# A planned two-layer RWKV-7/RetNet trunk: due-time schedules, ordered loads, and an inverse that reads its blocks from a padded copy in DRAM

## The chip, the cores and the metric

The kernel runs on one core of one Trainium2 chip. The metric is device time in microseconds (us), the median of several executions. Five engines matter: PE (TensorE, the matrix multiplier), DVE (VectorE), ACT (ScalarE), POOL (GpSimd) and SP (SyncE), which here only issues DMAs. Each engine works through its own instructions strictly in order; an instruction that waits holds up all that stand behind it on its engine, and a DMA that waits on SP holds up all later DMAs of SP.

## The reference

The input x is 256 tokens of 1024 features. Two layers each do

```
x += 1/2 swiglu(rms_norm(x))            # "f1"
h  = rms_norm(x);  proj = h @ w_in      # "mix": 1792 columns for RWKV, 1536 for RetNet
x += [rwkv7(proj_a) | retnet(proj_b)] @ w_out
x += 1/2 swiglu(rms_norm(x))            # "f2"
```

and a last rms_norm follows. swiglu is silu(h @ w_gate) * (h @ w_up) @ w_down with 2816 inner features. RWKV-7 has 8 heads of 64 and a state that each token updates: S <- S*diag(w) + (S a) b^T + v k^T, y = S r. The kernel does it in chunks of 64 tokens, and for each chunk and head it needs the inverse of a 64 x 64 unit triangular matrix. RetNet has 4 heads, with decay masks inside a chunk and between chunks.

## The kernel before

The 256 tokens are two tiles of 128, t0 and t1. Each runs as a stream of steps, and both share every weight: a weight half (128 x 1024 fp32, 512 KB) is loaded by SP into one of three raw buffers, ACT writes its rounded copy `hi`, DVE writes the remainder `lo`, and PE makes three products for each block (hi*hi, hi*lo, lo*hi). There are 332 halves: 66 for each f1, 34 for each mix (26 for the seven input projections, 8 for the output projection) and 66 for each f2. 22 places for hi and lo hold eleven halves at once.

In the mix the projections are m (decay, loras), k, r, q, e, g and v, in that order of loading; then come, for each tile: `R` (RetNet core), `J` (merge), `a` and `b` (the two chunks), `c` (closing norm) and the output projections `W` (RetNet half) and `w` (RWKV half). After r, `rwkv_receptance` forms the triangular matrices `el` (2 chunks x 4 head pairs, 128 partitions x 64 columns each) and calls `inverse`, which inverts their sixteen-wide diagonal blocks: the 64 blocks go through DRAM (`d1`) so that each comes to lie on one partition (`mx`), DVE doubles the inverted width from 2 to 4, 8 and 16, and the result goes back through DRAM (`d2`) into `xc`, which lies in the tile named misc. `merge` (J) joins the blocks to full inverses in four PE steps (`pre`), with ACT and DVE between them. Chunk steps a and b (`ch`) follow one another through the state `sv`; t1's follow t0's.

Nothing in this order is written by hand. The program is recorded as nodes, a planner (`Plan`) prices every node, computes each node's longest way to the end (`tails`), and simulates a list schedule with the priorities way + guide * position, for each of seven guides; the priorities with the earliest simulated end give the order in which every engine's instructions are emitted. A node that is recorded with `in_turn()` keeps its place among all nodes so marked; the weight loads are marked, the loads of x and of the constants are not.

Names in the rows: `base` holds x, constants, small vectors and the raw weight buffers; `wide` the hi and lo places; `parts` the normalized, transposed x; `gu` a bank for gate/up, projections and output projections; `acc` the banks of the down projection; `rh`, `rl` and `mh`, `ml` the inputs of W and w. Nearly all instructions carry the line of one helper, so the tiles tell them apart.

Of the kernel before, what the change touches and what calls it, by code (L numbers as in the profile page):

```python
# [21 lines left out]
P = 128  # L22
# [19 lines left out]
NPAIR = 4  # L42
# [108 lines left out]
class Op:  # L151
    __slots__ = ("eng", "call", "args", "kw", "outs", "ins", "cost", "late", "node", "at", "n", "form")


class Node:


    def __init__(self, eng):
        self.eng, self.ops, self.preds, self.succs = eng, [], {}, []
        self.touched = []  # L160
        self.dur = 0.0
        self.form = None


# [14 lines left out]
class Plan:  # L179
# [34 lines left out]
    def in_turn(self):  # L214

        n = self.nodes[-1]
        if self.turn is not None:
            n.preds.setdefault(self.turn, TURN)
        self.turn = n

    def record(self, eng, call, args, kw):
# [61 lines left out]
    def price(self, op):  # L283
# [36 lines left out]
        elif eng == "vector":  # L320
            if call == "tensor_tensor_scan":
                op.cost = 1224.0
            elif call in ("tensor_scalar", "tensor_copy", "memset") and not psum:
                op.cost = 150 + 0.52 * n
            elif call == "tensor_reduce":
                op.cost = 151 + 1.04 * int(np.prod(op.args[1].shape[1:]))
            elif len(out.shape) > 3 and out.shape[0] == 64:
                op.cost = 150 + 1.77 * n
            else:
                op.cost = 151 + 1.04 * n + (63 if col else 0)  # L330
        else:
            op.cost = 600.0 if call == "memset" else 450 + 190.0 * n
        op.cost += 20
# [14 lines left out]

    def tails(self, arcs):

        order = sorted(self.nodes, key=lambda n: (n.start, n.i)) if arcs else self.nodes
        tail = [0.0] * len(self.nodes)
        for n in reversed(order):
            best = n.dur
            for s, lag in n.succs:
                v = (60 if lag is TURN else lag) + tail[s.i]
                if v > best:
                    best = v
            for s, lag in (arcs.get(n.i, ()) if arcs else ()):
                v = (60 if lag is TURN else lag) + tail[s.i]  # L360
                if v > best:
                    best = v
            tail[n.i] = best
        return tail

    def simulate(self, prio):

        import heapq
        nodes = self.nodes
# [3 lines left out]
        state = {0: (128, 128), 2: "s"}  # L373
        lastnode = [None] * 5
        arcs = {}
        waiting = [[] for _ in range(5)]
        ready = [[] for _ in range(5)]
        places = {k: [(0.0, i, None) for i in range(n)] for k, (n, _) in PLACES.items()}
        left = {}
# [14 lines left out]
        while done < total:  # L394
# [6 lines left out]
            while pending and pending[0][0] <= t:  # L401
                ft, _, b, n = heapq.heappop(pending)
                places[b.space].append((ft, b.place, n))
            for e in range(5):
# [28 lines left out]
                for b in new:  # L433
                    pool = places[b.space]
                    j = min(range(len(pool)), key=lambda k: pool[k][0])
                    ft, b.place, prev = pool.pop(j)
                    if prev is not None:
                        arcs.setdefault(prev.i, []).append((n, max(1.0, ft - prev.start)))
                    low[b.space] = min(low.get(b.space, 99), len(pool))
# [11 lines left out]
                dur = n.dur + extra  # L451
                if lastnode[e] is not None:
                    arcs.setdefault(lastnode[e].i, []).append((n, t - lastnode[e].start if False else lastnode[e].real))
                lastnode[e] = n
                n.real = dur
# [25 lines left out]
                for b in n.touched:  # L481
                    b.last = max(b.last, fin + 60)
                    left[b.i] -= 1
                    if not left[b.i]:
                        heapq.heappush(pending, (b.last, b.i, b, n))
                        heapq.heappush(events, b.last)
        return end, arcs

    def schedule(self):

        self.prepare()
        way, n = self.tails(None), len(self.nodes)
        best = None
        for guide in GUIDES:
            prio = [w + guide * (n - i) * 1e5 / n for i, w in enumerate(way)]
            try:
                end, _ = self.simulate(prio)
            except Stuck:
                continue
            if best is None or end < best[0]:  # L500
                best = (end, prio)
            if VERBOSE:
                print(guide, end, self.low)
        self.end, _ = self.simulate(best[1])

# [38 lines left out]
class Trunk:  # L544
# [145 lines left out]
    def ffn(self, t, col, base, pause=()):  # L690
# [14 lines left out]
        for b in range(NB):  # L705
# [183 lines left out]
    def rwkv_receptance(self, t, ps):  # L889
# [12 lines left out]
        misc = A.get([P, 512], "misc")  # L902
        dg = misc[:, 0:128].rearrange("q (j p i) -> q j p i", j=2, p=NPAIR)
        for j in range(2):
# [7 lines left out]
            for h, q in enumerate((e, o)):  # L912
# [7 lines left out]
            lqs.append(lq)  # L920
            ld = A.get([P, NPAIR, 4, 16], "ld")
            TT(ld, el.rearrange("q p (b i) -> q p b i", b=4),
               self.c[:, C_BLK + 8:C_BLK + 72].rearrange("q (b i) -> q b i", b=4).unsqueeze(1).to_broadcast([P, NPAIR, 4, 16]),
               op=ALU.mult)
            nc.vector.tensor_reduce(dg[:, j], ld.rearrange("q p b i -> q p i b"), axis=AX.X, op=ALU.add)
            bs = A.get(full, "bs")
# [14 lines left out]
        ACT(bo, bps, AF.Copy)  # L941
        xc = self.inverse(t, dg, misc)
        z.update(lws=lws, lqs=lqs, bkt=bkt, el=el2, bo=bo, xc=xc)
# [28 lines left out]

    def inverse(self, t, dg, misc):

# [12 lines left out]
        xi = mx[0:64, n * n:].rearrange("u (s i) -> u s i", s=n)  # L987
        nc.gpsimd.memset(xi, 0.0)
# [4 lines left out]
        yi = misc[0:64, 256:320]  # L993
        for w in (2, 4, 8):
            sh = [64, w, w, w]
# [455 lines left out]
```

## Time and profile before

| | |
|---|---|
| median of three runs | 1106.56 us (1103.58 to 1111.81) |
| profiled execution, its own time | 1108.09 us |
| its span, first to last instruction | 1106.0 us |
| mean granted TensorE clock | 0.985 |
| PE busy | 1060.1 us (96%) |
| DVE busy | 668.8 us (60%) |
| ACT busy | 600.1 us (54%) |
| POOL busy | 36.8 us (3%) |
| DMA | 180.79 MB, mean 163 GB/s |

The busy time of PE is an overlap of pipelined matmuls, so it is close to the span everywhere but where PE truly stands still; how well it is used shows in matmuls per microsecond. The granted clock of 1.00 is 2.4 GHz and 0.50 is 1.2 GHz. The stages lie as follows in the span: f1 of layer 0 up to about 200 us, mix to 362, f2 and f1 of layer 1 to 740, mix to 902, f2 to 1098, and the closing norm.

### The profile page before, as it was taken

What the parts mean: (1) busy time and instruction counts of PE and PEld (TensorE: products, weight loads), DVE (VectorE), ACT (ScalarE), POOL (GpSimd) and SP (SyncE); (2) the same over time, 40 slices, a digit from 0 to 9 for tenths busy, and PEclk for the clock granted to TensorE, in tenths of its full rate; (3) what the DMA queues carried; (4) which work ended last, traced back from release to release, by engine and by line L of the source; (5) the groups of instructions that cost most, each with busy time, mean ns of one, the idle gap of its engine ahead of it and who ended that gap; (6) DMA issues with size and microseconds to landing.
All of it is one profiled execution on the core that took longest, in us unless ns stands there. A gap on an engine that the chain in (4) does not pass through costs nothing.

```text
span 1106.0 us, 16205 instructions
## 1 busy us (share of the span) xinstructions
PE 1060.1 (96%) x6253; PEld 861.2 (78%) x6253; DVE 668.8 (60%) x1107; ACT 600.1 (54%) x1012; POOL 36.8 (3%) x44
## 2 busy tenths in 40 slices
PE   7999999999989999999999999999969999999997
PEld 5778888887766788888888888878758777788886
DVE  5665454668867565555465545546887686655442
ACT  5554443775676654444364444447646865554431
POOL 0000000010010000000000000000100110000000
PEclk9999999999988999999999999999989999999999
DMA  6765556403544265546555554652137246655551
GB/s 232 236 213 195 186 177 215 160 29 113 170 140 142 79 207 189 191 163 213 178 174 187 185 189 161 214 202 78 32 112 217 64 143 201 202 197 172 176 166 39
DMA packets 59868, 180.79 MB, mean 163 GB/s; under 512 B 14352, under 2 KB 14992, under 8 KB 59792
## 3 DMA queue, kind: packets, MB, share of 16 engines
q1 hardware_dynamic: 59360, 179.63, 49.7%
q8 instruction: 49, 0.80, 0.3%
q14 instruction: 27, 0.22, 0.1%
q10 hardware_dynamic: 432, 0.13, 0.1%
HBM read 178.17 MB, written 1.57 MB: 163 GB/s over the span
## 4 chain that ended last, share of the span: by engine, by line
PE 76%; DMA 9%; ACT 7%; DVE 5%; issue 1%; POOL 0%; SPq 0%; POOLq 0%; ACTq 0%; DVEq 0%
PE gu L538 47%; PE acc L538 20%; DMA base<-in_w 7%; PE tr L538 5%; ACT wide L538 3%; DVE wide L538 2%; PE ch L538 2%; PE pre L538 1%; ACT parts L538 1%; DMA d<-misc 1%; DMA mx<-d 1%; DMA base<-in_x 0%; ACT junk L538 0%; DMA base<-in_consts 0%; DVE lw L538 0%
## 5 line engine op out<-in xcount | busy, mean ns | idle before, releaser
L538 PE MATMUL gu<-wide,parts 128*128 128x512 f32 (+1 forms) x2784 | 683.6, 394 | 15.6 <-DVE wide L538 10.7
L538 PEld LDWEIGHTS gu<-wide,parts 128*128 128x128 f32 x2784 | 511.4, 189 | 122.0 <-DVE wide L538 12.2
L538 DVE TENSOR_TENSOR wide<-base,wide 128x1024 fp32r<-128x1024 f32 x332 | 400.7, 1221 | 280.5 <-ACT wide L538 120.4
L538 ACT ACTIVATE wide<-base 128x1024 fp32r<-128x1024 f32 x332 | 350.6, 1060 | 340.5 <-DMA base<-in_w 175.0
L538 PE MATMUL acc<-wide,ht 128*128 128x512 f32 x1056 | 262.1, 392 | 0.0
L538 PEld LDWEIGHTS acc<-wide,ht 128*128 128x128 f32 x1056 | 197.4, 188 | 40.5 <-DVE ht L538 0.2
L538 POOL TENSOR_TENSOR base<-base 128x1 f32<-128x1 f32 (+2 forms) x26 | 32.1, 1234 | 1021.4 <-DVE base L538 1021.4
L538 DVE SCALAR_TENSOR_TENSOR hh<-gu,base,hh 128x256 f32<-128x256 f32 x88 | 40.2, 477 | 15.8 <-ACT hh L538 15.8
L538 DVE TENSOR_TENSOR ht<-tr,ht 128x256 fp32r<-128x256 f32 x88 | 34.4, 417 | 21.7 <-ACT ht L538 21.7
L538 ACT ACTIVATE ht<-tr 128x256 fp32r<-128x256 f32 x88 | 31.3, 377 | 26.7 <-PE tr L538 25.8
L538 ACT ACTIVATE hh<-gu,base 128x256 f32<-128x256 f32 x88 | 39.1, 464 | 11.2 <-PE gu L538 11.1
L538 DVE SCALAR_TENSOR_TENSOR parts<-tr,base,parts 128x128 fp32r<-128x128 f32 x96 | 29.2, 345 | 16.6 <-ACT parts L538 14.8
L538 ACT ACTIVATE parts<-tr,base 128x128 fp32r<-128x128 f32 x96 | 30.4, 375 | 15.9 <-PE tr L538 11.5
L538 PE MATMUL tr<-base,hh 128*128 128x128 f32 x176 | 32.8, 273 | 1.0 <-DVE ht L538 0.8
L538 PEld LDWEIGHTS tr<-base,hh 128*128 128x128 f32 x176 | 23.6, 140 | 11.2 <-DVE hh L538 1.8
L538 PE MATMUL tr<-base 128*128 128x128 f32 x96 | 18.6, 290 | 10.9 <-DMA base<-in_x 6.1
L538 ACT ACTIVATE junk<-base 128x1024 bf16<-128x1024 f32 (+1 forms) x16 | 15.2, 949 | 25.1 <-DVE base L538 25.1
L538 PEld LDWEIGHTS tr<-base 128*128 128x128 f32 x96 | 13.0, 146 | 17.8 <-ACT parts L538 8.2
L538 DVE SCALAR_TENSOR_TENSOR base<-acc,base 128x512 f32<-128x512 f32 x16 | 11.0, 687 | 24.1 <-PE acc L538 24.1
L538 PE MATMUL gu<-wide,rh 128*128 128x512 f32 x64 | 24.9, 434 | 0.2 <-ACT x L538 0.2
L538 DVE SCALAR_TENSOR_TENSOR shd<-tr,base,shd 128x127 f32<-128x127 f32 x56 | 17.8, 343 | 10.3 <-ACT shd L538 10.3
L538 PE MATMUL gu<-wide,mh 128*128 128x512 f32 x64 | 21.7, 414 | 1.3 <-ACT mh L538 1.3
(149 smaller groups left out, 612.0 us busy)
## 6 DMA issues: line engine op xcount, KB each, us to landing
base<-in_w SPq DMA_DIRECT2D x328, 512.0 KB, 4.4
base<-in_w SPq DMA_DIRECT2D x8, 256.0 KB, 4.6
lora<-in_lora SPq DMA_DIRECT2D x4, 256.0 KB, 4.5
out<-ot SPq DMA_DIRECT2D x4, 256.0 KB, 2.2
base<-in_consts SPq DMA_DIRECT2D x1, 805.0 KB, 7.4
base<-in_x SPq DMA_DIRECT2D x2, 256.0 KB, 5.1
base<-in_x SPq DMA_DIRECT2D x1, 512.0 KB, 5.9
fg<-in_fgain SPq DMA_DIRECT2D x2, 256.0 KB, 5.5
```

Of the source, the lines that this page charges most:

```text
L538: getattr(getattr(nc, op.eng), op.call)(*args, **kw)
```

## The change

The diff, cut to what the planner and the inverse do:

```diff
-GUIDES = (3, 5, 7, 10, 14, 20, 30)
+GUIDES = (5, 7, 10, 14, 20, 30)
+SERIES = 3
...
-            op.cost = 600.0 if call == "memset" else 450 + 190.0 * n
+            op.cost = 1100.0 if call == "memset" else 1000.0
...
-            best = n.dur
-            for s, lag in n.succs:
-                v = (60 if lag is TURN else lag) + tail[s.i]
...
+            tail[n.i] = max([n.dur] + [(60 if lag is TURN else lag + n.land) + tail[s.i] for s, lag in n.succs])
...
+    def deadlines(self, order):
+        due, t = [1e18] * len(self.nodes), 0.0
+        for n in order:
+            due[n.i] = t
+            t += n.real
+        for n in reversed(self.nodes):
+            for s, lag in n.succs:
+                d = due[s.i] - (60 if lag is TURN else lag + n.land)
+                if d < due[n.i]:
+                    due[n.i] = d
+        return due
...
             prio = [w + guide * (n - i) * 1e5 / n for i, w in enumerate(way)]
+            for k in range(SERIES):
+                try:
+                    end = self.simulate(prio)
+                except Stuck:
+                    break
+                if best is None or end < best[0]:
+                    best = (end, prio)
+                prio = [-d for d in self.deadlines(sorted((m for m in self.nodes if m.eng == 0), key=lambda m: m.start))]
...
             self.nc.sync.dma_start(self.x[t][:, w * n:w * n + w], self.x_d[t][:, w * n:w * n + w])
+            self.nc.in_turn()
...
                 nc.sync.dma_start(self.c[:, P:NCONST], self.consts_d[:, P:])
+                nc.in_turn()
...
-            ld = A.get([P, NPAIR, 4, 16], "ld")
-            TT(ld, el.rearrange("q p (b i) -> q p b i", b=4),
-               self.c[:, C_BLK + 8:C_BLK + 72]...to_broadcast([P, NPAIR, 4, 16]), op=ALU.mult)
-            nc.vector.tensor_reduce(dg[:, j], ld.rearrange("q p b i -> q p i b"), axis=AX.X, op=ALU.add)
...
-        d1 = self.A.dram([64, n * n], F32, name="d1")
+        d1 = self.A.dram([16, 4160], F32, name="d1")
...
-        nc.sync.dma_start(d1.rearrange(quads, b=8, s=n), dg.rearrange("q j p i -> q (j p) i"))
+        for h in range(2):
+            nc.sync.dma_start(d1.rearrange("(a h) n -> h a n", h=2)[h][:, 0:4096].rearrange("a (q x) -> q a x", x=64),
+                              els[64 * h:64 * h + 64].rearrange("q j p i -> q (j p) i"))
...
-        nc.sync.dma_start(m.rearrange("u s i -> u (s i)"), d1)
+        nc.sync.dma_start(m, d1.rearrange("g (c r) -> (g c) r", c=4)[:, 0:1024].rearrange("u (s x) -> u s x", x=64)[:, :, 0:16])
...
-        for w in (2, 4, 8):
+        for out, left, right in ((y2, small(m2, ur), small(x2, lr)), (small(x2, ur), small(x2, ul), y2)):
+            for k, q in enumerate((p2, q2)):
+                TT(q, left[:, :, :, k:k + 1].to_broadcast(sh), right[:, :, k:k + 1, :].to_broadcast(sh), op=ALU.mult)
+            TT(out, p2, q2, op=ALU.add)
+        for w in (4, 8):
```

So each guide now starts a series of three simulations: the second and third rank every node by a due time, counted back from the order that PE had in the one before. The landing time of a load counts in tails and due times. Loads of x and of the constants take their turn among the weight loads. In `inverse`, the four-way selection of diagonal blocks on DVE (`ld`, and its reduction) is gone; the whole of `el` is written to a DRAM copy whose rows of 4096 are padded to 4160, so that a step of 1040 leads from one diagonal block to the next and one DMA reads all blocks. The step to width 2 is six DVE instructions for all four pairs of a block where there were sixteen; the identity that grows into the inverse has a tile of its own (`mi`).

What the planner makes of it shows at three places. The first is SP at the start of the program (in_x is x, in_consts all constants but the identity). Before:

```order
L538 DMA base_63<-in_w 128x512 x6
L538 DMA base_63<-in_x 128x512 x2
L538 DMA base_63<-in_x 128x1024
L538 DMA base_63<-in_consts 128x1610
L538 DMA base_63<-in_w 128x512 x2
L538 DMA base_63<-in_w 128x1024 x62
```

and in the change:

```order
L544 DMA base_63<-in_x 128x512 x2
L544 DMA base_63<-in_w 128x512 x6
L544 DMA base_63<-in_x 128x1024
L544 DMA base_63<-in_w 128x512 x2
L544 DMA base_63<-in_w 128x1024 x28
L544 DMA base_63<-in_consts 128x1610
```

t0's x now leads, and the constants stand behind 32 weight halves instead of three.

The second is SP in the mix of layer 1, where each tile's inverse passes its four kinds of DMA (misc or el to d1, d1 to mx, mx or mi to d2, d2 to misc) among the weight loads. Before, from the last load of that layer's lora:

```order
L538 DMA base_63<-in_w 128x1024 x15
L538 DMA d1_1114_6334<-misc_1092_6295 128x8x16
L538 DMA base_63<-in_w 128x1024
L538 DMA mx_1116_6347<-d1_1114_6334 64x256
L538 DMA base_63<-in_w 128x1024
L538 DMA d2_1115_6470<-mx_1116_6347 64x256
L538 DMA d1_1149_6473<-misc_1127_6466 128x8x16
L538 DMA base_63<-in_w 128x1024
L538 DMA misc_1092_6295<-d2_1115_6470 128x8x16
```

and in the change:

```order
L544 DMA base_63<-in_w 128x1024 x25
L544 DMA d1_1110_6406<-el_1089_6382 64x8x64
L544 DMA base_63<-in_w 128x1024
L544 DMA d1_1110_6406<-el_1089_6382 64x8x64
L544 DMA base_63<-in_w 128x1024 x2
L544 DMA mx_1112_6466<-d1_1110_6406 64x16x16
L544 DMA base_63<-in_w 128x1024
L544 DMA d1_1144_6543<-el_1123_6530 64x8x64 x2
L544 DMA base_63<-in_w 128x1024
L544 DMA mx_1146_6592<-d1_1144_6543 64x16x16
L544 DMA d2_1111_6646<-mi_1113_6468 64x256
```

Before, 15 of the 26 projection halves stood ahead of the first DMA of t0's inverse; now 25 do, and all 26 stand ahead of the read of its blocks.

The third is the merge in layer 0, on DVE and on PE. On DVE (tc takes xc, the first read of the inverse's result; rsq is the last product of the RetNet core, rl the remainder for W) the rows were

```order
L538 TENSOR_SCALAR base_63<-base_63 128x4
L538 TENSOR_TENSOR wide18_83<-base_63,wide13_78 128x1024
L538 SCALAR_TENSOR_TENSOR shd_456_2419<-tr_455_2400,base_63,shd_456_2419 128x127
L538 SCALAR_TENSOR_TENSOR rsq_425_2438<-tr_424_2430,base_63,th_418_2268 128x128 x4
L538 SCALAR_TENSOR_TENSOR shd_456_2419<-tr_455_2400,base_63,shd_456_2419 128x127 x3
L538 TENSOR_TENSOR rl_428_2489<-tr_426_2476,rh_427_2485 128x512
L538 TENSOR_TENSOR tc_461_2491<-misc_320_1959,base_63 128x256
```

and are now

```order
L544 TENSOR_SCALAR low_460_2403<-misc_320_2202,base_63 128x128
L544 TENSOR_TENSOR prod_378_2319<-mx_376_2241,mi_377_2245 64x512
L544 SCALAR_TENSOR_TENSOR shd_454_2234<-tr_453_2225,base_63,shd_454_2234 128x127
L544 TENSOR_REDUCE misc_354_2334<-prod_378_2319 64x64
L544 SCALAR_TENSOR_TENSOR shd_454_2234<-tr_453_2225,base_63,shd_454_2234 128x127
L544 TENSOR_SCALAR base_63<-base_63 128x4
L544 TENSOR_TENSOR wide7_72<-base_63,wide2_67 128x1024
L544 SCALAR_TENSOR_TENSOR rsq_423_2409<-tr_422_2392,base_63,th_416_2153 128x128 x4
L544 TENSOR_TENSOR prod_378_2319<-mx_376_2241,mi_377_2245 64x512
L544 TENSOR_TENSOR tc_459_2368<-pre_463_2476,tc_459_2368 128x8x16
```

t0's xc is read (low, and tc seven rows above it) ahead of rsq instead of behind rl, and the tc that stands behind rsq is already the one after the merge's second step. On PE, t1's merge began behind all of t0's chunk b:

```order
L538 MATMUL ch_480_2796<-wt_479_2788,tt_460_2361 64x64 x8
L538 MATMUL tr_497_2793<-base_63,shd_496_2449 128x128 x3
L538 MATMUL gu_529_2753<-wide7_72,rh_449_2685 128x512
L538 MATMUL gu_529_2753<-wide0_65,rl_450_2719 128x512
L538 MATMUL ch_483_2773<-uv_459_2507,lq_330_1974 64x64 x8
L538 MATMUL ch_481_2828<-uv_459_2507,bkt_338_2025 64x64 x8
L538 MATMUL pre_506_2841<-tc_504_2805,el_354_2146 32x32 x32
```

and now its first step stands between the first and the second step of t0's chunk a:

```order
L544 MATMUL ch_474_2650<-sv_468_2526,lw_324_1954 64x64
L544 MATMUL ch_474_2650<-sv_468_2526,lw_325_2074 64x64
L544 MATMUL pre_504_2661<-tc_502_2622,el_353_2136 32x32 x32
L544 MATMUL ch_471_2699<-wt_470_2659,tt_458_2291 64x64 x8
L544 MATMUL gu_487_2558<-wide2_67,rl_426_2540 128x512
```

PE cannot go on with t0's chunk before t1's inverse has come back.

## Rows read from the trace of the kernel before

**Rows 1.** Stretches: length, busy us of PE, PEld, DVE, ACT, POOL; clock; DMA.
```profile
0.00:13.00 13.00, 4.83 (x15) 2.56 (x15) 5.30 (x13) 5.81 (x9) 0.20 (x4) 1.00 0.83 282
...
264.00:301.40 37.40, 35.27 (x181) 27.83 (x180) 32.48 (x81) 21.41 (x32) 0.54 (x1) 0.95 0.50 152
301.40:326.60 25.20, 20.38 (x309) 16.46 (x307) 17.52 (x38) 18.41 (x48) 3.86 (x4) 0.80 0.39 113
...
362.00:740.00 378.00, 377.03 (x1717) 309.02 (x1715) 208.21 (x270) 184.99 (x262) 4.77 (x5) 1.00 0.55 183
...
798.00:816.00 18.00, 8.61 (x60) 6.26 (x59) 15.52 (x49) 10.54 (x21) 0.00 (x0) 0.85 0.25 69
```
**Rows 2.** The chain that ended last, one piece: start us, us, what.
```profile
156.83 35.88 PE acc L538 x158
```
**Rows 3.** Timeline of the start: start us, us, engine, operation, tiles, count, idle before.
```profile
0.74 4.11 SPq L538 DMA_DIRECT2D base<-in_w  x6
...
4.89 1.38 SPq L538 DMA_DIRECT2D base<-in_x  x3
...
10.02 1.09 PE L538 MATMUL tr<-base 128*128 128x128 f32 x4 [6.10 <-DMA base<-in_x]
...
12.87 5.34 PE L538 MATMUL gu<-wide,parts 128*128 128x512 f32 x17
```
**Rows 4.** Waits on SP, one row: us in total, times, longest.
```profile
SPq L538 <- DVE misc L538: 19.6, 1, 19.6
```
**Rows 5.** Timeline of layer 1's mix, PE, DVE and SP.
```profile
798.13 0.38 SPq L538 DMA_DIRECT2D d<-misc  x1
...
799.80 1.45 PE L538 MATMUL gu<-wide,parts 128*128 128x512 f32 x5 [1.58 <-DVE wide L538]
...
808.11 1.06 ACT L538 ACTIVATE wide<-base 128x1024 fp32r<-128x1024 f32 x1
...
811.91 0.43 DVE L538 TENSOR_TENSOR ld<-el,base 128x256 f32<-128x256 f32 x1 [1.58 <-ACT el L538]
...
814.81 2.34 DVE L538 TENSOR_TENSOR wide<-base,wide 128x1024 fp32r<-128x1024 f32 x2
...
816.07 4.21 PE L538 MATMUL gu<-wide,parts 128*128 128x512 f32 x9 [7.89 <-DVE wide L538]
```
**Rows 6.** Busy time by stretch, one stretch of layer 1.
```profile
810.80:820.90 10.10, 4.83 (x13) 3.96 (x14) 7.91 (x11) 2.10 (x5) 0.00 (x0) 0.50 0.45 98
```
**Rows 7.** Timeline of layer 0's mix.
```profile
266.73 5.30 PE L538 MATMUL gu<-wide,parts 128*128 128x512 f32 x15 [1.78 <-ACT wide L538]
...
300.77 0.38 SPq L538 DMA_DIRECT2D misc<-d  x1
...
307.77 1.92 POOL L538 TENSOR_TENSOR base<-base 128x4 f32<-128x4 f32 x1 [24.08 <-DVE base L538]
...
312.66 0.42 DVE L538 TENSOR_TENSOR tc<-misc,base 128x256 f32<-128x256 f32 x1
...
336.31 0.75 PE L538 MATMUL pre<-tc,el 16*32 16x32 f32 x64
...
347.14 0.98 PE L538 MATMUL ch<-wt,tt 64*64 64x64 f32 x16 [0.56 <-ACT tt L538]
```
**Rows 8.** DMA issues: count, KB each, median us to landing.
```profile
d<-misc SPq DMA_DIRECT2D x4, 64.0 KB, 3.2
mx<-d SPq DMA_DIRECT2D x4, 64.0 KB, 2.9
...
misc<-d SPq DMA_DIRECT2D x4, 64.0 KB, 3.9
```
**Rows 9.** The tile ld: duration ns, least/median/most.
```profile
L538 DVE TENSOR_TENSOR ld<-el,base x8: 407/417/426, 249.5 to 811.9; 128x256 f32<-128x256 f32 x8
L538 DVE TENSOR_REDUCE misc<-ld x8: 561/587/603, 251.8 to 814.3; 128x64 f32<-128x256 f32 x8
```

**Rows 10.** Groups by form: busy us, mean ns of one, idle before.
```profile
L538 DVE TENSOR_TENSOR prod<-mx 64x8 f32<-64x8 f32 x16 | 1.5, 152 | 0.0
```

More of the change, by code (lines that the diff above doesn't have):

```diff
@@ L1 @@
+import heapq
 import math
@@ L151 @@
 class Op:
-    __slots__ = ("eng", "call", "args", "kw", "outs", "ins", "cost", "late", "node", "at", "n", "form")
+    pass
 class Node:
@@ L219, in in_turn, with behind @@
         self.turn = n
+    def behind(self, other):
+        self.nodes[-1].preds.setdefault(other, TURN)
     def record(self, eng, call, args, kw):
@@ L347, in prepare, with tails @@
                     u.touched.append(b)
-    def tails(self, arcs):
-        order = sorted(self.nodes, key=lambda n: (n.start, n.i)) if arcs else self.nodes
+    def tails(self):
         tail = [0.0] * len(self.nodes)
-        for n in reversed(order):
-            best = n.dur
-            for s, lag in n.succs:
-                v = (60 if lag is TURN else lag) + tail[s.i]
[L357 to L363, printed above, removed]
+        for n in reversed(self.nodes):
+            tail[n.i] = max([n.dur] + [(60 if lag is TURN else lag + n.land) + tail[s.i] for s, lag in n.succs])
         return tail
     def simulate(self, prio):
-        import heapq
         nodes = self.nodes
@@ L373, in simulate @@
         state = {0: (128, 128), 2: "s"}
-        lastnode = [None] * 5
-        arcs = {}
         waiting = [[] for _ in range(5)]
         ready = [[] for _ in range(5)]
-        places = {k: [(0.0, i, None) for i in range(n)] for k, (n, _) in PLACES.items()}
+        places = {k: [(0.0, i) for i in range(n)] for k, (n, _) in PLACES.items()}
         left = {}
@@ L435, in simulate @@
                     j = min(range(len(pool)), key=lambda k: pool[k][0])
-                    ft, b.place, prev = pool.pop(j)
-                    if prev is not None:
-                        arcs.setdefault(prev.i, []).append((n, max(1.0, ft - prev.start)))
+                    b.place = pool.pop(j)[1]
                     low[b.space] = min(low.get(b.space, 99), len(pool))
@@ L484, in simulate @@
                     if not left[b.i]:
-                        heapq.heappush(pending, (b.last, b.i, b, n))
+                        heapq.heappush(pending, (b.last, b.i, b))
                         heapq.heappush(events, b.last)
-        return end, arcs
+        return end
+    def deadlines(self, order):
[3 more added lines that the diff above has]
+            t += n.real
+        for n in reversed(self.nodes):
+            for s, lag in n.succs:
[3 more added lines that the diff above has]
+        return due
     def schedule(self):
         self.prepare()
-        way, n = self.tails(None), len(self.nodes)
+        way, n = self.tails(), len(self.nodes)
         best = None
@@ L941, in rwkv_receptance @@
         ACT(bo, bps, AF.Copy)
-        xc = self.inverse(t, dg, misc)
+        xc = self.inverse(t, el2, misc)
         z.update(lws=lws, lqs=lqs, bkt=bkt, el=el2, bo=bo, xc=xc)
@@ L971, in rwkv_value, with inverse @@
         z.update(uvs=uvs, v=v)
-    def inverse(self, t, dg, misc):
+    def inverse(self, t, els, misc):
         nc, A = self.nc, self.A
@@ L993, in inverse, with small @@
         yi = misc[0:64, 256:320]
-        for w in (2, 4, 8):
+        m2, x2 = (v[0:64, 0:272].rearrange("u (c y) -> u c y", c=4) for v in (mx, mi))
+        ul, ur, lr = (slice(o, o + 32) for o in (0, 2, 34))
+        def small(v, part):
+            return v[:, :, part].rearrange("u c (i y) -> u c i y", i=2)[:, :, :, 0:2]
+        y2, p2, q2 = (v.rearrange("u (c i j) -> u c i j", c=4, i=2) for v in (yi[:, 0:16], prod[0:64, 0:16], prod[0:64, 16:32]))
+        sh = [64, 4, 2, 2]
+        for out, left, right in ((y2, small(m2, ur), small(x2, lr)), (small(x2, ur), small(x2, ul), y2)):
[3 more added lines that the diff above has]
+        for w in (4, 8):
             sh = [64, w, w, w]
```

26 lines of the change are left out of this document (8 added, 18 removed).

## The prediction

> **What bounds the kernel now.** First the busy times by stretch. From 362 to 740 us PE is busy all but 1 us of 378, at the full clock [rows 1]; in the chain that ended last a piece of 158 matmuls takes 35.88 us, 0.227 us each [rows 2]. The change takes no matmul out, so those stretches, and all others in which PE has no gap, cost the same afterwards. What can move lies where PE stands still or has the lower clock. The reader is to see three such places. The first 13 us hold 4.83 us of PE [rows 1]. The mix of layer 0 has, from 301.4 to 326.6, 20.38 us of busy time in 25.2, at a mean clock of 0.80 [rows 1]. The mix of layer 1 has 8.61 us in the 18 from 798 to 816 [rows 1], and a clock of 0.50, which is 1.2 GHz, from 810.8 to 820.9 [rows 6]. Second come the waits in the timelines, which say who ends each gap; third, the order of the instructions before and after, for what now stands ahead of what. DVE, ACT and the DMAs have room on the whole, but on DVE and SP the order within the mix decides when a weight is ready, and so when PE may go on.
>
> **The change part by part.** The sum is made against the profiled execution, 1108.09 us, which is 1.5 us over the median of the three runs and 2.1 over its own span.
>
> *The start.* SP spends 4.11 us on six weight issues before it issues x at 4.89; PE waits 6.10 us for it and makes its first transposes at 10.02 [rows 3]. So x takes 5.1 us from issue to use. Issued first, at about 0.74, it allows transposes at 5.9, 4.1 us sooner. The long run of matmuls that begins at 12.87 [rows 3] follows the transposes by 2.85 us; its first weights now come behind x's two pieces, about 0.9 us later (two of three issues that take 1.38 [rows 3]), which that interval holds. The constants, 805 KB, no longer lie between the first three halves and the rest. I take 3 us of the 4.1, since the weights that follow pace t0's first block; ends: 0 (all is given back to loading) and 5.
>
> *The inverse itself.* Gone from DVE are eight `ld` of 0.42 us and eight reductions of 0.59 [rows 9], 8 us in four inverses; sixteen width-2 steps of 0.15 us for each tile [rows 10] become six of twice the width, which I put at 0.15 to 0.42 us, between that row and the one of `ld`. On the way to the result this saves about 1.0 us for each tile (one `ld` and its reduction). Against it the read of the blocks now takes 1024 pieces of 64 bytes where it took whole rows of 1 KB; the nearest rows are the DMA that reads in such rows, 2.9 us, and the one that reads in 64-byte pieces, 3.9 [rows 8], so 1.0 us more. The write moves four times the bytes in as many pieces, as two DMAs instead of one: between nothing and another 1.0, and one more issue of 0.38 us on SP [rows 5]. I put the inverse at 0, ends -2 and +4. The cover of that zero is that PE has projection matmuls while the inverse runs; where they run out, its length is on the path. The Trainium skill's "DMA: Bandwidth & Descriptors" (Specifications) says that a transfer needs pieces of at least 512 bytes to run at line rate, and that smaller ones are done as read-modify-write; it speaks against both new transfers, of 256 and of 64 bytes. By it write and read would each lose 1.0 us, for the one result in each layer that the chain waits for, and the sum below would be -11 instead of -15; but today's write, in 64-byte pieces, lands in 3.2 us where 1 KB rows take 2.9 [rows 8], so the trace shows 0.3 for pieces in that direction and I don't take the rule's price.
>
> *Mix of layer 0, before the merge.* PE waits 1.78 us at 266.73 for a weight [rows 7]; a mean clock of 0.95 over 37.4 us [rows 1] is 3.7 us at half clock, which costs about 1.9. In the changed order every projection half stands on SP ahead of the inverse. I take 2 us of these 3.7, ends 0 and 4.
>
> *Mix of layer 0, the merge.* t0's result was sent for at 300.77 [rows 7] and takes 3.9 us [rows 8], so it is there at 304.7; DVE reads it only at 312.66, since rsq ahead of it waits for a power on POOL that runs from 307.77 for 1.92 us [rows 7]. The 8.0 us between are what the new order, with this read ahead of rsq, can win at most. t1's merge begins at 336.31 and its chunk a makes its second step at 347.14 [rows 7]; those 10.8 us lie on the chain of chunks, and now they run beside t0's chunks. How much of either remains depends on the RetNet core, which is not shortened and which feeds the only filler. I take 6 us, nearer the lower end because PE still has the same work in the stretch; ends -3 (a loss) and 14.
>
> *Mix of layer 1.* SP stands 19.6 us at one DMA of the inverse [rows 4], the one issued at 798.13 [rows 5], with weight loads behind it. PE then waits 1.58 us at 799.80 and 7.89 us before 816.07 [rows 5]. The second of these ends with a DVE `wide` at 814.81, whose ACT half had begun at 808.11; ahead of it on DVE stood `ld`, itself waiting 1.58 us for ACT at 811.91 [rows 5]. `ld` is gone, and the 26 halves are called for before the inverse's read. With the gaps goes the half clock behind them: from 816.07 to 820.9 [rows 5, 6] PE lost about 2.4 us to it. Together 11.9; I take 9, ends 2 and 12.
>
> *New waits.* A simulated order meets real durations that differ from its prices, as in the 7.89 us above, which no planner would plan. The new order fits its prices more tightly: t1's merge now stands on PE inside t0's chunk a, and what is queued behind its first step is all of t0's chain. I charge 5 us for both layers; ends 2 (one gap like that at 799.80) and 14 (one like that before 816.07 with its half clock, and two small ones).
>
> The sum: -3 + 0 - 2 - 6 - 9 + 5 = -15, which makes 1093.1 of 1108.09, and 1091.6 on the scale of the median: **1092 us**.
>
> **The rivals.**
>
> *Bound by the chain, not by the order.* Merge, chunks a and b of t0, then of t1, then the closing norm follow one another in any order. If they and the RetNet core set the end of the mix, waits change places. For it: in 301.4 to 326.6 four engines have gaps at once [rows 1]. Against it: 8.0 us of waiting at t0's result come from order alone. Then the start and a third of layer 1's 9 are left, -6 and +2 for new waits: 1104 on the profiled scale, 1102 to 1103 on the median's. Range 1097 to 1108.
>
> *Slower: t1's inverse comes last.* In the new order PE reaches t1's first merge step before t0's chain may go on, and on SP the next weights stand behind the two DMAs that end t1's inverse. Its way is d1, the read, DVE, d2 and back: today the three DMAs with rows alone are 3.2, 2.9 and 3.9 us [rows 8], 10.0 together, and loads of 512 KB can stand before each. For it: SP's 19.6 us wait shows that such a DMA holds up the queue [rows 4]. Against it: from the end of the projections to that step the RetNet core needs time too, and the end of the inverse ran behind it in layer 0, by 8.0 us. If the result comes X us after PE gets there, X is lost in each layer, and about a third more at half clock, as 2.4 on 7.89. With X = 10 the two layers lose 27, and 1091.6 becomes 1118 to 1119. From X of 5.6 on (15 by twice 1.33) the kernel is slower than before, from 9.8 on by over 1%.
>
> *The change doesn't do what it says.* The series may let a first simulation, without due times, win, as before, and differ by chance; then only the start (3 us) and the inverse (0) are left: 1105, 1103 on the median's scale. The rows of the merge speak against it.
>
> **How the numbers follow.** A change of under 1%, 11 us, can't be told from none in a measurement here; the bounds are 1095.5 and 1117.6. My forecast has a chance of 0.55; its own range is 1077 (start 5, inverse 2, before the merge 2, merge 14, layer 1 at 12, new waits 5: -30, 1076.6 on the median's scale) to 1101 (new waits at 14: -6). Bound by the chain: 0.25. Not as it says: 0.08. Slower: 0.12. The range for 8 in 10 leaves out the lowest tail of the forecast and most of the slower rival: 1077 to 1109. Faster by over 1%: 0.50 of the forecast and 0.03 of the second, 0.53. Slower by over 1%: 0.10 of the slower rival and 0.01 of the rest, 0.11. Within 1%: 0.36.
>
> **What would show it.** In the profile of the changed kernel: the first transposes before 7 us; in layer 1's mix no PE wait for `wide` above 3 us, and SP nowhere held 10 us with projection weights behind it; DVE's first read of t0's result in layer 0 within 4 us of the last projection matmul, where it came 11.3 us after (301.4 to 312.66 [rows 1, 7]); less time at half clock in both mixes. It would be wrong if a PE row shows `pre` waiting over 5 us for DVE `tc`, if SP's longest wait is a DMA of t1's inverse with f2's weights behind, or if the RetNet core's rsq stays the last releaser and the stretch from the projections' end to f2 keeps its length.

## The result and the profile after

The changed kernel takes 1099.19 us (median of five executions, 1095.67 to 1101.27); the kernel before, timed beside it, 1109.38. The ratio is 0.9897, with a 95% interval of 0.9863 to 0.9930: about 11 us less, near the bound of 1% and below the 15 us that were forecast, which lie at the edge of the interval. The profiled execution is the slowest of the five, 1101.27 us with a span of 1099.4, where before had 1108.09 and 1106.0; between these two traces only 6.6 us of span lie, and the accounts by stage below are of these 6.6.

Busy time by stretch of the changed kernel (length; busy us of PE, PEld, DVE, ACT, POOL; clock; DMA share, GB/s), for the stretches of [rows 1] and of [rows 6]:

```profile
0.00:13.00 13.00, 6.99 (x19) 4.00 (x20) 5.75 (x18) 6.96 (x14) 0.20 (x4) 1.00 0.71 228
...
264.00:301.40 37.40, 37.40 (x216) 30.69 (x215) 29.22 (x69) 26.13 (x52) 1.38 (x5) 0.96 0.35 92
301.40:326.60 25.20, 22.55 (x405) 18.05 (x401) 16.86 (x46) 15.22 (x42) 4.78 (x4) 0.93 0.16 44
...
362.00:740.00 378.00, 372.55 (x1674) 301.24 (x1673) 206.67 (x264) 182.81 (x255) 3.12 (x4) 1.00 0.57 184
...
798.00:816.00 18.00, 17.39 (x94) 13.84 (x93) 15.62 (x22) 9.84 (x15) 0.00 (x0) 1.00 0.56 181
810.80:820.90 10.10, 10.10 (x66) 7.97 (x66) 9.08 (x14) 9.08 (x17) 0.43 (x2) 1.00 0.72 206
```

Where before stood still, PE now works: 6.99 us in the first 13 instead of 4.83, 17.39 from 798 to 816 instead of 8.61, and from 810.8 to 820.9 the clock is 1.00 instead of 0.50. The stretches of the FFNs (the f1 and f2 stages) tell the other half. From 362 to 740 PE was full before (377.03); now it is busy for 372.55 us. And at the end of layer 0's f1, from 190 to 220 us, before and after:

```profile
190.00:220.00 30.00, 29.78 (x169) 24.50 (x169) 21.15 (x40) 20.77 (x46) 2.02 (x2) 1.00 0.53 173
```

```profile
190.00:220.00 30.00, 26.64 (x137) 20.50 (x136) 16.80 (x26) 15.09 (x27) 1.46 (x1) 0.94 0.50 167
```

PE does 32 matmuls fewer there, at a mean clock of 0.94 where it was 1.00.

Milestones of the same work in both traces give the account. Each is the start of the last or first matmul of its kind; the last column is what the stage gained or lost. At the end of an f1 the first matmuls of the mix run already, so the border between the two is not sharp.

| | before | after | stage |
|---|---|---|---|
| first matmul of the first long run | 11.6 | 9.8 | -1.8 |
| last down-projection matmul of layer 0's f1 | 211.0 | 217.1 | **+7.9** |
| last output matmul of layer 0's mix | 377.1 | 372.9 | -10.3 |
| last down-projection matmul of layer 1's f1 | 753.3 | 755.5 | **+6.4** |
| last output matmul of layer 1's mix | 915.0 | 908.3 | -8.9 |
| last down-projection matmul of f2 | 1098.7 | 1091.0 | -1.0 |
| end of the span | 1106.0 | 1099.4 | +1.1 |

So the two mixes gain 10.3 and 8.9 us, and the FFNs around them lose 7.9 and 6.4.

The start, as a timeline (start us, us, engine, operation, tiles, count, idle before), against [rows 3]:

```profile
0.73 0.87 SPq L544 DMA_DIRECT2D base<-in_x  x2
...
5.10 1.94 PE L544 MATMUL tr<-base 128*128 128x128 f32 x8 [1.18 <-DMA base<-in_consts]
...
8.69 1.05 ACT L544 ACTIVATE wide<-base 128x1024 fp32r<-128x1024 f32 x1
...
9.80 0.79 PE L544 MATMUL gu<-wide,parts 128*128 128x512 f32 x1 [2.76 <-ACT wide L544]
...
11.06 2.50 PE L544 MATMUL gu<-wide,parts 128*128 128x512 f32 x5 [0.47 <-DVE wide L544]
```

The transposes come 4.9 us sooner (5.10 for 10.02), but PE then waits 2.76 us for the first weight copy, which ACT begins at 8.69, so that the run of matmuls gains 1.8 (9.80 for 11.57).

Layer 0's merge, where [rows 7] had t0's result read late:

```profile
298.35 0.38 SPq L544 DMA_DIRECT2D misc<-d  x1
...
302.33 0.41 DVE L544 TENSOR_TENSOR tc<-misc,base 128x256 f32<-128x256 f32 x1
...
309.50 0.75 PE L544 MATMUL pre<-tc,el 16*32 16x32 f32 x64
...
310.29 1.92 POOL L544 TENSOR_TENSOR base<-base 128x4 f32<-128x4 f32 x1 [17.84 <-DVE base L544]
...
312.25 1.13 DVE L544 SCALAR_TENSOR_TENSOR rsq<-tr,base,th 128x128 f32<-128x128 f32 x4 [0.91 <-POOL base L544]
...
314.29 0.28 DVE L544 TENSOR_TENSOR tc<-pre,tc 128x128 f32<-128x128 f32 x1
...
325.97 0.68 PE L544 MATMUL ch<-wt,tt 64*64 64x64 f32 x16
...
340.69 0.68 PE L544 MATMUL ch<-wt,tt 64*64 64x64 f32 x16
```

DVE reads t0's result at 302.33 instead of 312.66. PE takes the first merge step only at 309.50, and the second read on DVE, at 314.29, stands behind the same rsq that waits for the same power on POOL. Chunk a of t0 makes its second step at 325.97; before, it was 326.6. What gains is t1: its merge begins at 325.29, between two steps of t0's chunk a, where it was 336.31, and its chunk a makes its second step at 340.69 for 347.14 [rows 7].

One reading of [rows 7] has to be put right. The DMA at 300.77 brings t1's result, not t0's: in the planned order of the kernel before, t0's inverse is the first of the two on SP, and its result was sent for at

```profile
276.02 0.39 SPq L538 DMA_DIRECT2D misc<-d  x1
```

By the 3.9 us of [rows 8] it was there at about 280, some 33 us before DVE read it at 312.66. In the changed kernel the DMA at 298.35 is t0's.

The new loss holds three stalls of one kind, two at the end of layer 0's f1 and one between layer 0's f2 and layer 1's f1. The rows are of ACT and PE:

```profile
195.72 1.06 ACT L544 ACTIVATE wide<-base 128x1024 fp32r<-128x1024 f32 x1 [1.29 <-DMA base<-in_w]
196.69 0.61 ACT L544 ACTIVATE parts<-tr,base 128x128 fp32r<-128x128 f32 x2
...
197.74 0.33 PE L544 MATMUL tr<-base 128*128 128x128 f32 x1 [1.70 <-DVE parts L544]
...
212.44 1.06 ACT L544 ACTIVATE wide<-base 128x1024 fp32r<-128x1024 f32 x1 [2.19 <-DMA base<-in_w]
213.40 0.46 ACT L544 ACTIVATE tok<-gu,base 128x256 f32<-128x256 f32 x1
213.91 0.33 PE L544 MATMUL tr<-base,tok 128*128 128x128 f32 x1 [1.42 <-ACT tok L544]
...
564.61 1.06 ACT L544 ACTIVATE wide<-base 128x1024 fp32r<-128x1024 f32 x1 [1.74 <-DMA base<-in_w]
565.57 0.35 ACT L544 ACTIVATE parts<-tr,base 128x128 fp32r<-128x128 f32 x1
565.97 0.33 PE L544 MATMUL tr<-base 128*128 128x128 f32 x1 [2.13 <-ACT parts L544]
```

Each time ACT stands at a weight copy whose load has not landed. Behind it, in order, stands the read of a PSUM bank for which PE waits. The waits name `parts` and `tok`, which ACT writes as it reads those banks; what held ACT is the DMA one row earlier. The three waits are 5.3 us of the 14.3 that the FFNs lost; the rest was not followed wait by wait.

### The profile page after: what moved, and what is told of

Same layout as the page of the kernel before. It is cut to its first block, busy times and chain, and to the rows that moved or that the text cites. A ratio compares the mean times of both kernels' runs of the same rounds, so it can differ in the third digit from the quotient of the medians.

```text
span 1099.4 us, 16122 instructions
## 1 busy us (share of the span) xinstructions
PE 1062.5 (97%) x6253; PEld 853.3 (78%) x6253; DVE 661.4 (60%) x1051; ACT 599.1 (54%) x1012; POOL 38.1 (3%) x44
## 2 busy tenths in 40 slices
DMA packets 63772, 181.57 MB, mean 165 GB/s; under 512 B 18512, under 2 KB 18896, under 8 KB 63696
## 3 DMA queue, kind: packets, MB, share of 16 engines
q1 hardware_dynamic: 63264, 180.42, 50.8%
## 4 chain that ended last, share of the span: by engine, by line
PE 66%; DMA 15%; DVE 7%; ACT 5%; issue 5%; POOL 1%; ACTq 0%; POOLq 0%; DVEq 0%; SPq 0%
PE gu L544 39%; PE acc L544 19%; DMA base<-in_w 14%; PE tr L544 5%; DVE wide L544 4%; ACT wide L544 4%; PE ch L544 2%; PE pre L544 1%; POOL base L544 1%; ACT parts L544 1%; DMA base<-in_vecs 1%; DMA mx<-d 1%; DVE parts L544 0%; DMA d<-el 0%; ACT junk L544 0%
## 5 line engine op out<-in xcount | busy, mean ns | idle before, releaser
L544 PE MATMUL gu<-wide,parts 128*128 128x512 f32 (+1 forms) x2784 | 702.7, 396 | 8.0 <-ACT wide L544 2.8
L544 PE MATMUL acc<-wide,ht 128*128 128x512 f32 x1056 | 279.8, 396 | 0.7 <-ACT wide L544 0.6
L544 DVE TENSOR_TENSOR ht<-tr,ht 128x256 fp32r<-128x256 f32 x88 | 37.0, 420 | 90.6 <-ACT ht L544 90.5
L544 ACT ACTIVATE parts<-tr,base 128x128 fp32r<-128x128 f32 x96 | 31.8, 365 | 31.7 <-PE tr L544 22.0
L544 PE MATMUL tr<-base,hh 128*128 128x128 f32 x176 | 43.3, 272 | 0.3 <-DVE ht L544 0.3
L544 PE MATMUL tr<-base 128*128 128x128 f32 x96 | 23.2, 302 | 7.3 <-ACT parts L544 3.4
L544 ACT ACTIVATE junk<-base 128x1024 bf16<-128x1024 f32 (+1 forms) x16 | 15.1, 945 | 24.8 <-DVE base L544 24.8
```

Of the source, the lines that this page charges most:

```text
L544: getattr(getattr(nc, op.eng), op.call)(*args, **kw)
```

## The experiments

The planner of this kernel computes a simulated end for the order that it chooses, and the chip can be held against it. For before it is 1075.2, for the changed kernel 1045.3: a promise of 29.9 us, of which the chip kept 11. The theories at first: A, the order by due times carries the gain; B, the inverse carries it; C, the chip keeps what the plan promises. In the table "promise" is the change of the simulated end against before, "measured" the ratio less one times 1111 us. Before itself chose guide 20. Each kernel is one order that its planner chose, so two rows differ by their edit and by all that the planner moves with it.

| kernel | ratio, 95% interval | promise | measured |
|---|---|---|---|
| changed kernel (guide 7, due times) | 0.9897 (0.9863 to 0.9930) | -29.9 | -11 |
| inverse alone (chose guide 30) | 0.9851 (0.9815 to 0.9887) | -14.2 | -17 |
| planner alone (chose guide 30, due times) | 0.9966 (0.9945 to 0.9987) | -19.3 | -4 |
| no due times (chose guide 30) | 0.9834 (0.9800 to 0.9868) | -17.0 | -18 |
| ordered loads alone (chose guide 20) | 0.9971 (0.9948 to 0.9994) | -1.7 | -3 |
| before, guide 30 | 0.9985 (0.9964 to 1.0005) | +0.2 | -2 |
| due times, guide 30 | 0.9936 (0.9915 to 0.9957) | -27.4 | -7 |
| no due times, guide 7 | 0.9988 (0.9965 to 1.0011) | -15.8 | -1 |
| inverse without width 2 at once, guide 30 | 0.9995 (0.9970 to 1.0021) | -5.7 | -1 |
| due times, guide 30, landing priced | 0.9765 (0.9725 to 0.9805) | -24.8 | -26 |
| due times, guide 30, banks counted | 0.9813 (0.9778 to 0.9849) | -28.5 | -21 |
| both of these | **0.9708** (0.9677 to 0.9739) | -26.8 | **-32** |
| no due times, guide 30, landing priced | 0.9763 (0.9727 to 0.9799) | -12.1 | -26 |

**The inverse alone.** `inverse` and `rwkv_receptance` of the changed kernel in the kernel before; nothing of `Plan` changes.

> The kernel before with the new inverse alone (padded copy in DRAM, width 2 for all blocks at once, no ld); the planner, its prices and the order of x's loads as before. Theory A, the order carries the gain and the inverse only little of it: 3 us off, ratio 0.995 to 1.000. Rival B, the shorter chain of the inverse carries it: 8 us or more off, ratio 0.993 or less. Rival C, the plan's own arithmetic is kept by the chip: its simulated end falls from 1075.2 to 1061.0, so 14 us off, ratio 0.987.

0.9851: theory A falls here, B and C both stand. The inverse did not get shorter from end to end. From the first write to the last landing it took 23.7, 22.2, 22.3 and 26.7 us before, and 27.3, 28.4, 26.2 and 28.4 here. What it frees is DVE, 56 instructions and 7 us in the page of the changed kernel (661.4 us of busy time in 1051 instructions, 668.8 in 1107 before), and the planner then chooses another order.

**The planner alone.** The old inverse in the changed kernel.

> The changed kernel with the inverse of before (rows of 1 KB in DRAM, ld and its reductions, width 2 block by block); planner, prices and ordered loads as changed. Theory A, the order carries the gain: 8 us off, ratio 0.991 to 0.994, and SP again stands long at the inverse's DMAs less than 10 us with projection weights behind. Rival B, the inverse carries it: only the start is left, 2 us off, ratio 0.997 to 1.000. Rival C, the plan's arithmetic is kept: its simulated end is 1055.9 where before had 1075.2, 19 us off, ratio 0.983.

0.9966, no more than the ordered loads by themselves (0.9971, below). This is B's number, and C, which expected 0.983, falls.

**Without due times.**

```
-SERIES = 3
+SERIES = 1
```

> The changed kernel with one simulation for each guide, so no order by due times; inverse, prices and ordered loads as changed. Theory A in the form that due times carry the gain: 4 us off, ratio 0.995 to 0.999, with layer 0's read of t0's inverse late again (over 8 us after its DMA was issued). Rival B, the inverse carries it: 8 us or more off, ratio 0.993 or less. Rival C, the plan's arithmetic is kept: 1058.2 against 1075.2, 17 us off, ratio 0.985.

0.9834, better than the changed kernel, though the two intervals touch. The read of t0's result is late by the sign that was set, 21.8 us after its DMA at 279.01; but it comes at 300.82, no later than in the changed kernel (302.33).

**The ordered loads alone.** In the kernel before:

```
             self.nc.sync.dma_start(self.x[t]...)
+            self.nc.in_turn()
...
                 nc.sync.dma_start(self.c[:, P:NCONST], self.consts_d[:, P:])
+                nc.in_turn()
```

> The kernel before with x and the constants put in the order of the weight loads and nothing else. If the start is worth what the changed kernel's first long run of matmuls shows (at 9.8 us where it was 11.6), 2 us off, ratio 0.998, and the first matmuls of that run at about 9.8. If it is given back to the weights that now come behind x: none, with the run's first 60 us as long as before. Rival C, the plan's arithmetic: 1073.5 against 1075.2, 2 us off.

0.9971, 3 us: the start is worth what was said, and the first long run begins at 8.8.

So far the new inverse seems to carry everything, and due times to cost 0.6%. But the two faster kernels both use guide 30 and the changed kernel guide 7, so the value from GUIDES had to be taken out.

**Before with guide 30.** `GUIDES = (30,)`.

> The kernel before, its planner held to guide 30, the one that the planner chose for the new inverse alone; the chosen one of before is 20. Theory D, the new inverse itself brings the 1.5%: the simulated end stays (1075.4 against 1075.2), so ratio 0.997 to 1.003. Rival E, it is the other guide's order that brought it and the inverse little: ratio 0.985 to 0.992.

0.9985, as theory D expected: guide 30 alone does nothing for the old inverse.

**Due times with guide 30.** In the changed kernel:

```
-GUIDES = (5, 7, 10, 14, 20, 30)
-SERIES = 3
+GUIDES = (30,)
+SERIES = 2
```

> The changed kernel held to guide 30 with one round of due times: the run with one round for each guide (0.9834) chose guide 30 without them. Theory F, due times themselves cost time on the chip, since they leave no slack: ratio 0.987 to 0.994. Rival G, due times are harmless and guide 7, which the changed kernel chose, is a bad order: ratio 0.984 or less. The plan's arithmetic: 1047.8 against 1058.2 without due times, so 10 us less, 0.974.

0.9936, in the range of theory F: at guide 30 due times cost 1.0%. And with them the new inverse is worth little: planner alone, the same guide and due times with the old inverse, has 0.9966, so 0.3%, and the intervals overlap. With the planner of before it was 1.3% at guide 30 (0.9985 to 0.9851). What the inverse brings depends on the order around it. The profile says where the due times lose. PE's waits in the FFNs of layers 0 and 1 (372 to 770 us; total, times, longest) are led by one row,

```profile
PE tr L544 <- DVE ht L544: 8.1, 4, 4.0
```

and the longest of the four looks so on ACT, DVE and PE:

```profile
422.41 0.39 PE L544 MATMUL tr<-base,hh 128*128 128x128 f32 x2
...
424.88 1.06 ACT L544 ACTIVATE wide<-base 128x1024 fp32r<-128x1024 f32 x1 [2.19 <-DMA base<-in_w]
426.12 1.06 ACT L544 ACTIVATE wide<-base 128x1024 fp32r<-128x1024 f32 x1 [0.18 <-DMA base<-in_w]
427.08 0.37 ACT L544 ACTIVATE ht<-tr 128x256 fp32r<-128x256 f32 x1
427.48 0.42 DVE L544 TENSOR_TENSOR ht<-tr,ht 128x256 fp32r<-128x256 f32 x1 [3.53 <-ACT ht L544]
427.95 0.47 PE L544 MATMUL tr<-base,hh 128*128 128x128 f32 x1 [4.01 <-DVE ht L544]
```

The transposes that end by 422.80 wait to be read by ACT. ACT idles 2.19 us at a weight copy, does two copies, and only then reads them; PE's next transposes wait for that bank.

**Guide 7 without due times.** `GUIDES = (7,)`, `SERIES = 1`.

> The changed kernel held to guide 7 without due times; the changed kernel itself is guide 7 with one round of them. Theory F: ratio 0.981 to 0.986, 4 to 9 us below the changed kernel. Rival G: ratio 0.988 to 0.993, as the changed kernel. The plan's arithmetic: 1059.4, 1.2 more than guide 30's.

0.9988: neither F nor G. At guide 7 the due times gain 0.9%, at guide 30 they lose 1.0%. PE's largest waits here are for `wide` 6.0 us, `sc` 5.7 and `tok` 4.0. Without due times the two guides lie 1.5% apart on the chip, with simulated ends of 1058.2 and 1059.4; the simulated end does not tell the good order from the bad.

**The padded copy without the new width 2.** The kernel before with guide 30 and the new inverse, with one line back:

```
-        for w in (4, 8):
+        for w in (2, 4, 8):        # and without the step for all blocks at once
```

> The kernel before, guide 30, with the padded copy in DRAM and without ld, but width 2 still block by block. If ld and its place on DVE carry the gain of the inverse: ratio 0.985 to 0.990. If the 40 small instructions that width 2 saves carry it: 0.994 to 1.000. The plan's arithmetic: 1069.5 against 1075.4 of guide 30 and 1061.0 of the full new inverse, so 0.995.

0.9995, as expected if width 2 carries the gain: the padded copy and the missing ld bring nothing that can be measured at guide 30; with width 2 for all blocks at once it is 0.9851. One place in the trace, DVE and PE:

```profile
280.94 0.17 DVE L538 COPY mi<-mx 64x8 f32<-64x8 f32 x1 [3.07 <-DMA mx<-d]
...
281.62 0.38 DVE L538 TENSOR_TENSOR prod<-mx,mi 64x8 f32<-64x8 f32 x4
...
282.77 1.20 DVE L538 TENSOR_TENSOR wide<-base,wide 128x1024 fp32r<-128x1024 f32 x1
...
284.03 2.50 PE L538 MATMUL gu<-wide,parts 128*128 128x512 f32 x5 [4.02 <-DVE wide L538]
```

Again an engine stands at an instruction whose DMA is late, here the inverse's read, and the weight behind it makes PE wait. The inverse alone has a stall of the same kind there (DVE 2.76 us, PE 2.85), so this place accounts for little of what parts the two kernels. How much of the 16 us between them comes from the ten instructions that width 2 no longer issues in each inverse, and how much from the other order that the planner then chooses, is not separated by these runs.

Stalls of one kind on two engines make a theory. The planner prices a load's landing at its size over 330 bytes per ns plus 1.7 us, which is 3.3 us for a weight. The trace of the changed kernel has, for its 327 weight loads from 14 us on, all of 512 KB:

```profile
DMA to landing us min/median/max: 3.5/4.4/7.6
```

Theory L: the price is below even the least, so copies are planned ahead of PSUM reads for data that is not there yet. Its rival is a new B, of the banks: due times see who needs a read's data, not who needs its bank.

**Landing priced.**

```
-land = fabric + (1700.0 if size > 70000 else 2100.0)
+land = fabric + (2800.0 if size > 70000 else 2100.0)
```

> The kernel with guide 30 and one round of due times (measured at 0.9936, where guide 30 without due times had 0.9834), its planner now pricing the fixed part of a large DMA at 2.8 us instead of 1.7; a weight load of 512 KB is then planned at 4.4 us, the median that the traces show. Theory L, due times lose because weight copies on ACT are planned ahead of PSUM reads for data that lands later than priced: ratio 0.981 to 0.988, and PE's waits for ht in the FFNs, 8.1 us in four, fall below 2 us. Rival B, due times lose because they don't count the PSUM bank that a read frees: ratio 0.991 to 0.996, the waits stay. The plan's arithmetic: 1050.4 against 1047.8, no gain.

0.9765, better than L expected, and the waits for ht in the FFNs are gone. They were 8.1 us in all; another part of the gain lies from 30 to 70 us, where PE is busy for 40.00 us of 40 instead of 36.20. One row shows what the price does, ACT's weight copies and the idle time before them, with due times at guide 30 before and after the new price:

```profile
L544 ACT ACTIVATE wide<-base 128x1024 fp32r<-128x1024 f32 x332 | 350.6, 1060 | 332.4 <-DMA base<-in_w 207.2 <-PE acc L544 58.8 <-PE gu L544 50.4
```

```profile
L544 ACT ACTIVATE wide<-base 128x1024 fp32r<-128x1024 f32 x332 | 349.4, 1060 | 264.6 <-PE acc L544 94.3 <-DMA base<-in_w 90.0 <-PE gu L544 70.5
```

The work is the same 350 us; ACT stands 90.0 us at loads instead of 207.2. This total is not the cost itself: the inverse alone has 249.0 us of it at 0.9851, and before has 175.0. It costs where a read that PE needs stands behind the copy.

**Banks counted.** In `deadlines`:

```
+            for b in n.touched:
+                if b.space == "bank" and n.eng:
+                    w = max((due[u.i] + u.dur for u in b.users if u.eng == 0 and u.i < n.i), default=1e18)
+                    due[n.i] = min(due[n.i], w + 1500.0)
```

> The kernel with guide 30 and one round of due times, landing as priced before, but with due times that also count PSUM banks: what reads a bank on ACT or DVE is due at the latest 1.5 us after the last matmul into it. Theory B: ratio 0.981 to 0.988, and PE's waits for ht in the FFNs below 2 us. Rival L: ratio 0.991 to 0.996, since ACT still stands at a copy whose load has not landed. The plan's arithmetic: 1046.7, about as without it.

0.9813: the ratio that B expected, so the banks are a condition of the stall too. ACT still stands 203.5 us at loads, but PE's waits for ht in the FFNs are down to one of 1.0 us: what stands behind the copies is no longer what PE needs first.

**Both.**

> Both at once: landing priced at 2.8 us and due times that count PSUM banks, guide 30. If each removes a part of the same waits (theory L and B are two conditions of one stall): ratio 0.980 to 0.986, at most a little under the better of the two alone. If due times cost for a third reason: 0.990 or more, as without either. The plan's arithmetic: 1048.4.

0.9708, 1079.12 us (1077.43 to 1081.64): 32 us below before and about 20 below the changed kernel, the best of all runs and more than was expected of both at once. The stretch from 362 to 740 is full again:

```profile
362.00:740.00 378.00, 376.72 (x1730) 309.19 (x1728) 214.95 (x273) 189.17 (x269) 3.12 (x4) 1.00 0.57 188
```

**Landing priced, no due times.** The same price with `SERIES = 1`.

> Guide 30 without due times, landing priced at 2.8 us: the run with due times at this price had 0.9765, guide 30 without due times at the old price 0.9834. Theory M, due times gain once the price is right, so that they turn from +1.0% into a gain: ratio 0.981 to 0.990, and the four waits of PE for ht or hh in the FFNs come to 1 to 5 us. Rival N, the price alone did it and due times add nothing: ratio 0.973 to 0.979. The plan's arithmetic: 1063.1 without due times against 1050.4 with, so 12 us or 1.1% for due times.

0.9763, the same as with due times: theory M falls, N holds. At a price of 2.8 us due times add nothing by themselves. With banks counted they have 0.9708 against 0.9763; the intervals overlap a little, so their gain of 0.5% is likely, not shown. The new price itself is worth 1.7% with due times (0.9936 to 0.9765) and 0.7% without (0.9834 to 0.9763), both at guide 30; no other guide was tried with it.

## Why the prediction was right or wrong

The sum was 15 us less, and the ratio gives 11. That the total came near is in part luck. The forecast gave 15 to the order and nothing to the inverse; alone, the order brings 4 (planner alone) and the inverse 17. By its steps:

- *Start, -3.* Right: -3 us alone, and -1.8 at the first long run. The loss is where it was looked for, at the weights behind x.
- *The inverse itself, 0 (-2 to +4).* The step that failed, as to which part of the change carries the gain. As a length on the path the value was right, even kind. But its cover was judged in the order of before, as if 56 instructions fewer left that order alone. With the planner of before, this part alone makes the kernel 17 us faster; with due times at the same guide it is 3, not shown apart from noise. The term had to be asked as "what else may the planner do then", not as "how much sooner is the result".
- *The pieces of the inverse's DMAs.* The Trainium skill's "DMA: Bandwidth & Descriptors" (Specifications) asks for pieces of at least 512 bytes for line rate. For the write the trace doesn't bear out the 1.0 us that the forecast gave to this rule: in 256-byte pieces it lands in 2.5 us, where the old one in 64-byte pieces took 3.2 [rows 8]. For the read the runs come near it: in 64-byte pieces its medians are 3.2 us in the changed kernel and 3.0 to 5.2 over the ten kernels that have it, where rows of 1 KB took 2.9 to 3.6 over the other four. Each median is of four transfers. The 0.3 us by which the forecast set the rule aside compares a write with a read; the old write in rows took 2.6, so it should have been 0.6:

```profile
d<-mx SPq DMA_DIRECT2D x4, 64.0 KB, 2.6
```

- *Layer 0, before the merge and at it, -2 and -6.* About right in size: the mix is 10.3 us shorter, with a border at f1 that is not sharp. The half that was counted on t1, whose merge now runs beside t0's chunks, came: its chunk a is 6.4 us sooner. The half that was counted on t0 did not. The read came 3 us before the last projection matmul, as was said, but the next read of the same chain fell behind the same rsq and the same POOL power of 1.92 us, so t0's chunk gained 0.6 us. The 8.0 us that were put at that read were t1's DMA misread as t0's. So the rival "bound by the chain" held for t0's first chunk, not for the mix. And the early read is not the due times' doing: the inverse alone, with the planner of before, has it at 302.32.
- *Layer 1, -9.* Right: -8.9, with the 7.89 us wait and its half clock gone.
- *New waits, +5.* Right in kind, too small and wrong in place. They were looked for in the mixes; 7.9 and 6.4 us came in the FFNs, 14.3 together, at the end of the range that was given (14). The FFNs were said to cost the same because PE had no gap there. A stretch without gaps is covered by its order, and the order changed.
- *The slower rival.* Its sign showed without its price: SP stands 19.1 us at the inverse of t1, in layer 1, its longest wait but for the 31.7 us at the output, with the last half of the output projection and f2's weights behind it. But that result had landed at 863.97 and PE began t1's merge at 869.92, so X was below zero. The wait, as in [rows 4]:

```profile
SPq L544 <- DVE mi L544: 28.8, 4, 19.1
```

What was not asked at all is how far the planner's prices are from the trace. Rows of the kernel before have the landing of a weight at 4.4 us where the code prices 3.3. At guide 30 the correction of this 1.1 us is worth 1.7% with due times (0.9936 to 0.9765), 19 us and more than the whole change, and 0.7% without. The change's new price for POOL, 1.0 us for any power, is off as well, against 0.76 to 2.10 us in the trace; what that costs was not tried.

## What to carry to other kernels

Where a planner sets the order, judge a change by the planner's prices against the trace: on an in-order engine a price that is too low can become a stall of whatever stands behind, as at the weight copies here, and a tighter plan can pay more for it. Price a load by the usual landing under load, not by the least, and let what frees a PSUM bank be due by the bank; both paid here, at the one guide where they were tried. An account by stages needs a border at every stage: a gain of 10.3 us and a loss of 7.9 look like 2.4 when f1 and the mix are taken together. Measure a planned change at several of its orders: here due times cost 1.0% at one guide and gained 0.9% at another.

## What was not expected of the hardware

A weight load of 512 KB lands in 3.5 us at the least, 4.4 in the median and 7.6 at the most, though one queue carries 180.42 of the 181.57 MB. The Trainium skill's "DMA: Bandwidth & Descriptors" (Anatomy of one DMA) gives, for DMAs that GpSimd issues, about 2.0 us plus the bytes over 436 GB/s; worked out, an estimate, 3.2 us. The trace, where SP issues the loads, agrees with that as a floor: the least lies 0.3 us above it and the median 1.2, and a price near that floor is what theory L turned on. And a power on POOL costs 0.76 us for one column, 1.46 for four and 2.10 for eight in the changed kernel (0.81, 1.33 and 1.92 in the kernel before); by form, busy us and mean ns:

```profile
L544 POOL TENSOR_TENSOR base<-base 128x8 f32<-128x8 f32 x8 | 16.8, 2095 | 110.4 <-DVE base L544 110.4
L544 POOL TENSOR_TENSOR base<-base 128x1 f32<-128x1 f32 x14 | 10.6, 756 | 816.6 <-DVE base L544 816.6
L544 POOL TENSOR_TENSOR base<-base 128x4 f32<-128x4 f32 x4 | 5.9, 1464 | 50.3 <-DVE base L544 50.3
```
